# Sums of squares in a decoder layer: 128x128 blocks turned on TensorE and added on VectorE instead of float32 products with ones

## The chip, the cores and the metric

The kernel runs on one core of a Trainium2 chip. The metric is the device time of one execution in microseconds (us), and a version is judged by the median of its runs. The core has a matrix engine (TensorE, "PE" in the profile, with its weight loads shown apart as "PEld"), a vector engine (VectorE, "DVE"), a scalar engine (ScalarE, "ACT"), a general engine (GpSimd, "POOL") and a queue that mostly issues transfers (SyncE, "SP"). Each engine takes its instructions strictly in its own order, and they wait for one another by semaphores.

## What is computed

One layer of a decoder over 1024 tokens with 1024 features, all in float32:

```
x = x + 1/2 * SwiGLU_1(RMSNorm(x))
h = RMSNorm(x); z = h @ W_in      # [u | v | c_q | c_kv | k_rope | q_mem | gates]
merged = sum_i sigmoid(gate_i) * (y_i @ W_branch_i)     # gating, latent and memory attention
x = x + merged @ W_out
x = x + 1/2 * SwiGLU_2(RMSNorm(x))
```

What matters here are the root-mean-square norms, `x * rsqrt(mean(x*x) + EPS) * g`. Each needs, for every token, the sum of the squares over some features:

- over the 1024 features of `x`, in three places: before the first feed-forward block ("ffn1"), before the mixer's input projection ("mix") and before the second feed-forward block ("ffn2");
- over the 1024 features of the 256 memory tokens (`mem`);
- over the 128 features of each of four query heads of the memory attention (`q_mem`);
- over the 384 features of the low-rank query `c_q` (the kernel adds 256 of them at the place that is changed here, and the last 128 elsewhere).

## The kernel before

**Layout.** Activations lie feature by feature: a tile has 128 features on the partitions and tokens along the row, so the tokens are handled in two halves of 512. The sum over features runs across partitions. The squares are first added up, feature tile by feature tile, into one tile (128 features by tokens), and what remains is a sum over 128 partitions for each token.

**How that sum is made.** `token_sums` (line 391) does it on TensorE. For each block of 128 tokens it takes the 128x128 block of squares as the stationary operand and one column of ones (`self.ones`) as the moving one, in plain float32, and gets one column of 128 sums in a PSUM bank, one token on each partition. In the trace each such float32 product is recorded as two weight loads and two matmuls. `query_roots` (line 762) does the same with `self.pick`, a 128x2 matrix whose first column has ones in the upper 64 rows and whose second column has them in the lower 64, because its tile holds two heads of 64 summed features each. The sums go, straight from PSUM, into `rms` (line 206): nine small VectorE instructions (lines 192 and 169 to 185) that compute the reciprocal root.

**The way back.** Where the root has to multiply features-by-tokens tiles, `norm_scale` (line 405) spreads it with TensorE transposes (line 411): each takes a root column, broadcast to 128x128, as the stationary operand and the identity `self.ident` as the moving one. Transposes of this kind also occur in many other places (lines 436, 614, 818, 922, 1006, 1041).

**Main products.** All large products are split into three (`mm3`, lines 155 to 161): each float32 operand becomes a rounded high part and a rest, made by a ScalarE copy and a VectorE subtraction (lines 139 and 142; the profile also shows them as 146 and 147, and as 150 and 151 with a gain), and three matmuls of 512 columns (lines 158, 159, 160) are added in PSUM. A scheme with seven products in place of eight (class `Seven`) adds VectorE sums of weights (line 1411) and of results (line 1439).

**Order of the work.** Three kinds of stages matter:

- The ffn blocks' second half (`down`) and the first units after it run under an order written out by hand, for TensorE, VectorE and ScalarE, and in `down` for SyncE too.
- The input projection (`Gates.run`, line 1664) goes through fifteen units of seven products each. There only TensorE's order is written by hand; the other engines' order is made by a planner that simulates a timeline. After the first product of some units the table `sums` calls `mem_root` (unit 2), `query_roots` (units 7 and 10) and `latent_sums` (unit 12). The squares of these come from stored values that are read back, squared on ScalarE and added on GpSimd (`squares`, line 663), one unit or more earlier.
- The mixer and the output projection (`project`, line 1114) are planned throughout.

**PSUM.** There are eight banks of 512 columns: a ring of four called `bank` (line 135), which the sums use, and four more that `single` or `mm` use. Each unit of the projection takes one `bank` and two `single`.

**Who calls `token_sums`.** `OpNorm.tokens` (line 1288) for both halves of the three norms of `x` (with `late`, which puts the first matmul behind the latest main product in TensorE's order), `mem_root` with 2 blocks, `latent_sums` with 8. For the mix norm, `tokens(0)` and `root` stand ahead of step (5, 2) of `down`, and `turn`, which calls `norm_scale`, ahead of step (5, 3). For ffn2, `first` (line 1326) is called by `project` after the first output tile of the second half.

Of the kernel before, what the change touches and what calls it, by code (L numbers as in the profile page):

```python
# [8 lines left out]
F32 = mybir.dt.float32  # L9
# [4 lines left out]
ALU = mybir.AluOpType  # L14
AXX = mybir.AxisListType.X

P = 128
D = 1024
S = 1024
DT = D // P  # L20
NT = S // P
# [13 lines left out]
ML = 256  # L35
# [14 lines left out]
class Kernel:  # L50
# [193 lines left out]
    def late_constants(self):  # L244

        nc, a, const = self.nc, self.a, self.const

        def load(name, shape):
            t = const.tile(shape, F32, name="c_" + name)
            nc.sync.dma_start(t, a[name])  # L250
            return t

        self.b_gate = load("b_gate", [P, 3 * DT])
        self.g_mix, self.g_ffn2, self.g_mem = (load(n + "_norm", [P, DT]) for n in ("mix", "ffn2", "mem"))
        self.g_cq = load("mla_cq_norm", [P, QR // P])
        self.sg_b = load("sg_b", [P, SGG])
        self.mq_g = load("mem_q_norm", [P, 1])
        self.mk_g = load("mem_k_norm", [P, 1])
        self.gq_m = const.tile([P, 1], F32, name="gq_m")
        nc.gpsimd.tensor_scalar(self.gq_m, self.mq_g, -MD ** -0.5, None, op0=ALU.mult)  # L260
        self.pick = const.tile([P, 2], F32, name="pick")
        nc.gpsimd.memset(self.pick, 0.0)
        for o in range(2):
            nc.gpsimd.memset(self.pick[o * P // 2:(o + 1) * P // 2, o:o + 1], 1.0)
        self.g_ev = {}
        rope_g = {}
        for n in ("q", "k"):
            g = const.tile([QK, 1], F32, name=f"g_ev_{n}")
            nc.gpsimd.memset(g, 1.0)
            nc.sync.dma_start(g[:NOPE], a[f"mla_{n}_norm"][:NOPE].unsqueeze(1))  # L270
            self.g_ev[n] = g
            rope_g[n] = const.tile([P, ROPE], F32, name=f"rope_g_{n}")
            nc.sync.dma_start(rope_g[n], a[f"mla_{n}_norm"][NOPE:].partition_broadcast(P))
        pos = const.tile([P, NT], I32, name="pos_i")
        nc.sync.dma_start(pos, a["positions"])
        inv = const.tile([P, ROPE // 2], F32, name="inv")
        nc.sync.dma_start(inv, a["inv_freq"].partition_broadcast(P))
        yield
        yield from self.rope_tables(rope_g, pos, inv)
# [111 lines left out]
    def token_sums(self, acc, late=False, bank=None, more=()):  # L391


        n = acc.shape[-1] // P
        b = (bank or self.bank)()[:, :n]
        for t in range(n):
            for m, x in enumerate((acc, *more)):
                i = self.nc.tensor.matmul(
                    b[:, t:t + 1], x[:, t * P:(t + 1) * P], self.ones, start=m == 0, stop=m == len(more))
                if late and t == m == 0:  # L400
                    self.after(i, self.last)
        self.final = i
        return b

    def norm_scale(self, r, late=False, bank=None):


        n = r.shape[-1]
        b = (bank or self.bank)()
        for t in range(n):  # L410
            i = self.nc.tensor.transpose(
                b[:, t * P:(t + 1) * P], r[:, t:t + 1].to_broadcast([P, P]), self.ident)
            if late and t == 0:
                self.after(i, self.last)
        self.final = i
        return b[:, :n * P]
# [332 lines left out]
    def mem_root(self, t):  # L749

        v, row = self.nc.vector, self.row()
        v.tensor_tensor(row, t[:, :512], t[:, 512:], op=ALU.add)
        v.tensor_tensor(row[:, :ML], row[:, :ML], row[:, ML:], op=ALU.add)
        self.m_r = self.const.tile([P, ML // P], F32, name="m_r")
        v.tensor_copy(self.m_r, self.rms(self.token_sums(row[:, :ML]), ML // P, D))

    def query_squares(self, z, pair):

# [3 lines left out]
    def query_roots(self, pair, t):  # L762

        nc = self.nc
        b = self.bank()[:, :NT * 2]
        for n in range(NT):
            nc.tensor.matmul(b[:, 2 * n:2 * n + 2], t[:, n * P:(n + 1) * P], self.pick, start=True, stop=True)
        if pair == 0:
            self.mq_r, self.mq_nr = (
                self.const.tile([P, NT * MH], F32, name=n).rearrange("p (t h) -> p t h", h=MH) for n in ("mq_r", "mq_nr"))  # L770
        c = slice(2 * pair, 2 * pair + 2)
        nc.vector.tensor_copy(self.mq_r[:, :, c], self.rms(b, NT * 2, MD).rearrange("p (t h) -> p t h", h=2))
        nc.gpsimd.tensor_scalar(self.mq_nr[:, :, c], self.mq_r[:, :, c], -1.0, None, op0=ALU.mult)
# [5 lines left out]
    def latent_sums(self, t):  # L779

        self.cq_s = self.const.tile([P, NT], F32, name="cq_s")
        self.nc.vector.tensor_copy(self.cq_s, self.token_sums(t))

    def mem_rows(self):

# [466 lines left out]
class OpNorm:  # L1252
# [35 lines left out]
    def tokens(self, half):  # L1288
        k = self.k
        more, self.more = self.more, []  # L1290
        self.s[half] = k.token_sums(self.acc.pop(half), late=k.last is not None, more=more)

    def root(self, half):
        self.r[half] = self.k.rms(self.s[half], 4, D)
# [1005 lines left out]
```

## Time and profile before

| | |
|---|---|
| Median of 3 runs | 2167.88 us (2167.59 to 2170.26) |
| Profiled execution, first to last instruction | 2168.8 us (of this execution no other time is recorded) |
| Granted TensorE clock, mean | 0.999 |
| Busy TensorE / weight loads | 2159.0 us (100%) / 1804.2 us (83%) |
| Busy VectorE / ScalarE / GpSimd | 1567.5 us (72%) / 912.3 us (42%) / 256.9 us (12%) |
| DMA, mean share of 16 engines, on the hardware queue | 45.4% |

A row of the page or of a timeline gives the start, the duration, the engine, the line of the kernel, the operation, the output and inputs with their shapes, a count, and in brackets how long the engine stood idle before it and what released it. Matmuls overlap: the duration of one is longer than the distance from one start to the next, so what an insertion costs TensorE is read from the starts.

### The profile page before, as it was taken

The numbers are of one execution on the slowest core, as the hardware profiler recorded it, in microseconds if no ns is written. First come the engines' busy times: TensorE is split into PE (matmuls) and PEld (weight loads), VectorE is DVE, ScalarE is ACT, GpSimd is POOL, SyncE is SP. The second block draws the span as 40 slices with busy tenths as digits, with TensorE's granted clock in tenths as the row PEclk, the third lists the DMA queues.
The fourth block names the chain that finished last, engine by engine and source line by source line (L and its number), as shares of the span: only waits on it lengthen the run. The fifth ranks groups of instructions, "written<-read, shape, count | busy, mean of one in ns | idle before, by whom it ended". The sixth has DMA issues, their size and how long they took to land.

```text
span 2168.8 us, 27547 instructions
## 1 busy us (share of the span) xinstructions
PE 2159.0 (100%) x10170; PEld 1804.2 (83%) x10170; DVE 1567.5 (72%) x2362; ACT 912.3 (42%) x1492; POOL 256.9 (12%) x271
## 2 busy tenths in 40 slices
PE   9999999999999999999999999999999999999999
PEld 6888888888887888888888899988888888888887
DVE  7966666679889656655786679886886666657884
ACT  5433333333455434433555378833432232224332
POOL 0011111100000000000133321240011211110000
PEclk9999999999999999999999999999999999999999
DMA  4264555385332445641577821193033333338443
GB/s 147 92 219 160 187 180 175 123 319 189 123 116 100 145 164 174 223 148 61 209 279 260 312 101 60 51 354 110 34 132 102 103 99 99 108 138 289 169 130 104
DMA packets 129975, 340.98 MB, mean 157 GB/s; under 512 B 15280, under 2 KB 23600, under 8 KB 129840
## 3 DMA queue, kind: packets, MB, share of 16 engines
q1 hardware_dynamic: 129696, 339.21, 45.4%
q8 instruction: 80, 1.31, 0.2%
q14 instruction: 55, 0.45, 0.1%
q10 hardware_dynamic: 144, 0.00, 0.0%
HBM read 229.33 MB, written 109.84 MB: 156 GB/s over the span
## 4 chain that ended last, share of the span: by engine, by line
PE 93%; DVE 4%; ACT 1%; DMA 1%; issue 1%; SPq 0%; ACTq 0%; DVEq 0%
PE one L158 15%; PE one L159 15%; PE one L160 15%; PE bank L158 13%; PE bank L159 12%; PE bank L160 12%; PE mm L158 2%; PE mm L159 2%; PE mm L160 2%; PE bank L1006 1%; PE bank L1021 1%; PE bank L1022 1%; PE bank L436 1%; PE one L1935 1%; DVE w L147 1%; DVE wlo L147 1%
## 5 line engine op out<-in xcount | busy, mean ns | idle before, releaser
L146 ACT CAST whi<-x 128x1024 fp32r<-128x1024 f32 x202 | 192.2, 955 | 419.0 <-DVE x L1411 169.9
L147 DVE TENSOR_TENSOR wlo<-x,whi 128x1024 fp32r<-128x1024 f32 x202 | 241.1, 1195 | 58.8 <-ACT whi L146 21.0
L1439 DVE TENSOR_TENSOR t<-t,one 128x512 f32<-128x512 f32 x188 | 128.8, 685 | 195.2 <-PE one L160 195.1
L158 PE MATMUL bank<-h,whi 128*128 128x512 f32 x636 | 247.9, 390 | 0.0
L160 PE MATMUL bank<-h,wlo 128*128 128x512 f32 x636 | 247.6, 389 | 0.0
L159 PE MATMUL bank<-h,whi 128*128 128x512 f32 x636 | 247.6, 389 | 0.0
L158 PE MATMUL one<-h,whi 128*128 128x512 f32 x508 | 199.2, 392 | 0.0
L159 PE MATMUL one<-h,whi 128*128 128x512 f32 x508 | 198.2, 390 | 0.0
L160 PE MATMUL one<-h,wlo 128*128 128x512 f32 x508 | 198.2, 390 | 0.0
L158 PE MATMUL one<-w,whi 128*128 128x512 f32 x432 | 168.8, 391 | 0.1
L160 PE MATMUL one<-w,wlo 128*128 128x512 f32 x432 | 168.2, 389 | 0.0
L159 PE MATMUL one<-w,whi 128*128 128x512 f32 x432 | 168.1, 389 | 0.0
L142 DVE TENSOR_TENSOR wlo<-w,whi 128x1024 fp32r<-128x1024 f32 (+2 forms) x112 | 114.4, 1037 | 67.1 <-ACT whi L139 66.9
L139 ACT CAST whi<-w 128x1024 fp32r<-128x1024 f32 (+2 forms) x112 | 98.8, 902 | 149.8 <-PE one L159 63.9
L2035 POOL TENSOR_TENSOR raw<-raw 128x512 f32<-128x512 f32 x38 | 56.9, 1498 | 794.1 <-DVE raw L1876 684.1
L160 PEld LDWEIGHTS bank<-h,wlo 128*128 128x128 f32 x636 | 119.4, 188 | 24.9
L158 PEld LDWEIGHTS bank<-h,whi 128*128 128x128 f32 x636 | 119.4, 188 | 24.6
L159 PEld LDWEIGHTS bank<-h,whi 128*128 128x128 f32 x636 | 119.4, 188 | 24.4
L160 PE MATMUL bank<-whi,wlo 128*128 128x512 f32 x352 | 137.0, 389 | 0.0
L158 PE MATMUL bank<-whi 128*128 128x512 f32 x352 | 137.0, 389 | 0.0
L159 PE MATMUL bank<-wlo,whi 128*128 128x512 f32 x352 | 137.0, 389 | 0.0
L158 PEld LDWEIGHTS one<-h,whi 128*128 128x128 f32 x508 | 95.8, 189 | 20.0 <-issue 0.2
(406 smaller groups left out, 4904.7 us busy)
## 6 DMA issues: line engine op xcount, KB each, us to landing
x<-in_ffn_w_gu_dram SPq DMA_DIRECT2D x78, 512.0 KB, 5.1
w<-tdt SPq DMA_DIRECT2D x40, 512.0 KB, 4.5
gate<-raw SPq DMA_DIRECT2D x33, 512.0 KB, 2.9
tdb<-raw SPq DMA_DIRECT2D x64, 256.0 KB, 2.3
h<-in_ffn_w_down_dram SPq DMA_DIRECT2D x64, 256.0 KB, 6.2
w<-tdb SPq DMA_DIRECT2D x30, 512.0 KB, 4.6
tdt<-w SPq DMA_DIRECT2D x48, 256.0 KB, 2.3
x<-in_w_gate_dram SPq DMA_DIRECT2D x22, 512.0 KB, 7.0
```

Source lines behind the costliest of these rows:

```text
L139: i = self.nc.scalar.copy(hi, src)
L142: return (eng or self.nc.vector).tensor_tensor(lo, src, hi.bitcast(F32), op=ALU.subtract)
L146: self.nc.scalar.copy(hi, src)
L147: return lambda: self.nc.vector.tensor_tensor(lo, src, hi.bitcast(F32), op=ALU.subtract)
L158: i = mmul(out, s[0], m[0], start=first, stop=False, **kw)
L159: mmul(out, s[0], m[1], start=False, stop=False, **kw)
L160: self.last = mmul(out, s[1], m[0], start=False, stop=last, **kw)
L436: nc.tensor.transpose(b[:m, k * P:(k + 1) * P], s, self.ident)
L1006: nc.tensor.transpose(b[:, at:at + P], prs[t][:, kk * P:(kk + 1) * P], self.ident)
L1021: nc.tensor.matmul(o, w, pt[0], start=n == 0, stop=False)
L1439: return self.nc.vector.tensor_tensor(out, x, y, op=ALU.add)
L2035: sub = lambda d, x, y: (eng or nc.gpsimd).tensor_tensor(d, x, y, op=ALU.subtract)
```

## The change

A new helper, `turned_sums`, takes the place of the float32 products in five calls: `mem_root` (2 blocks), the two calls of `query_roots` (8 blocks each), `latent_sums` (8 blocks), and `tokens(0)` of the mix norm and of the ffn2 norm (4 blocks each). Each 128x128 block of squares is transposed on TensorE into a PSUM bank, four blocks to a bank, and one VectorE reduction for each bank adds along the row: over 128 features, or over twice 64 for the query heads (`parts=2`). The sums now lie in an SBUF tile ("ts"). Eight blocks take two banks where they took one. The ffn1 norm, whose object is made with `scaled=True`, and `tokens(1)` of the other two keep `token_sums`. `self.pick` and its three GpSimd memsets go.

```diff
-        self.pick = const.tile([P, 2], F32, name="pick")
-        nc.gpsimd.memset(self.pick, 0.0)
-        for o in range(2):
-            nc.gpsimd.memset(self.pick[o * P // 2:(o + 1) * P // 2, o:o + 1], 1.0)
...
+    def turned_sums(self, acc, parts=1, late=False):
+        nc, n = self.nc, acc.shape[-1] // P
+        out = self.stat("ts", NT * 2)[:, :n * parts]
+        for t0 in range(0, n, 4):
+            m = min(4, n - t0)
+            b = self.bank()
+            for t in range(m):
+                i = nc.tensor.transpose(b[:, t * P:(t + 1) * P], acc[:, (t0 + t) * P:(t0 + t + 1) * P], self.ident)
+                if late and t0 == t == 0:
+                    self.after(i, self.last)
+            nc.vector.tensor_reduce(
+                out[:, t0 * parts:(t0 + m) * parts],
+                b[:, :m * P].rearrange("p (x d) -> p x d", d=P // parts), axis=AXX, op=ALU.add)
+        self.final = i
+        return out
...
-        v.tensor_copy(self.m_r, self.rms(self.token_sums(row[:, :ML]), ML // P, D))
+        v.tensor_copy(self.m_r, self.rms(self.turned_sums(row[:, :ML]), ML // P, D))
...
-        b = self.bank()[:, :NT * 2]
-        for n in range(NT):
-            nc.tensor.matmul(b[:, 2 * n:2 * n + 2], t[:, n * P:(n + 1) * P], self.pick, start=True, stop=True)
+        b = self.turned_sums(t, 2)
...
-        self.nc.vector.tensor_copy(self.cq_s, self.token_sums(t))
+        self.nc.vector.tensor_copy(self.cq_s, self.turned_sums(t))
...
-        self.s[half] = k.token_sums(self.acc.pop(half), late=k.last is not None, more=more)
+        if half == 0 and not self.scaled:
+            self.s[half] = k.turned_sums(self.acc.pop(half), late=True)
+        else:
+            self.s[half] = k.token_sums(self.acc.pop(half), late=k.last is not None, more=more)
```

## The prediction

> **What bounds the kernel now.** I read the page's sums first, then the chain of work that ended last, then what TensorE waits for.
>
> ```profile
> span 2168.8 us, 27547 instructions
> PE 2159.0 (100%) x10170; PEld 1804.2 (83%) x10170; DVE 1567.5 (72%) x2362; ACT 912.3 (42%) x1492; POOL 256.9 (12%) x271
> ...
> PE 93%; DVE 4%; ACT 1%; DMA 1%; issue 1%; SPq 0%; ACTq 0%; DVEq 0%
> ```
>
> ```profile
> PE bank L231 <- POOL pick L264: 1.5, 1, 1.5
> PE bank L1935 <- DVE x L1911: 1.2, 2, 0.7
> ...
> PE bank L411 <- DVE rs_y L185: 0.7, 1, 0.7
> ```
>
> TensorE is busy for all but 9.8 us of the span, and 93% of the chain runs through it. The first wait is the start of the program; the one at line 411 is at a half norm that the change leaves alone. So what shortens TensorE's own list of instructions shortens the time, as long as no other engine becomes late. By stage (columns: stretch, length, busy time and count of PE, PEld, DVE, ACT and POOL, clock, DMA share, GB/s), the input projection and, for later use, the two parts of the mixer:
>
> ```profile
> 700.00:960.00 260.00, 259.91 (x1175) 215.64 (x1174) 162.40 (x229) 106.83 (x132) 10.96 (x6) 1.00 0.51 173
> ...
> 1060.00:1240.00 180.00, 179.43 (x991) 158.05 (x990) 137.13 (x285) 92.82 (x228) 55.55 (x62) 1.00 0.77 277
> 1240.00:1420.00 180.00, 179.24 (x1216) 162.98 (x1215) 151.42 (x317) 137.48 (x304) 42.36 (x96) 1.00 0.28 102
> ```
>
> In the projection, where 26 of the 34 replaced blocks are, TensorE has 0.1 us of idle time in 260, and VectorE has 98 us to spare.
>
> **What is removed.** 34 blocks: 2 (memory), 8 and 8 (queries), 8 (latent), 4 (mix norm), 4 (ffn2 norm). Of each, two recorded matmuls go. The query sums (line 767) and the latent sums (the whi form of line 398):
>
> ```profile
> L767 PE MATMUL bank<-pick,whi x32: 165/251/252, 850.3 to 911.1; 128*128 128x2 f32 x32
> ...
> L398 PE MATMUL bank<-ones,whi x16: 164/250/251, 949.4 to 951.0; 128*128 128x1 f32 x16
> ```
>
> The durations overlap, so I go by the starts of TensorE's main matmuls around a place. The first query sum:
>
> ```profile
> 848.05 0.39 PE L160 MATMUL bank<-h,wlo 128*128 128x512 f32 x1
> ...
> 850.09 0.39 PE L160 MATMUL bank<-h,wlo 128*128 128x512 f32 x1
> ...
> 850.32 1.84 PE L767 MATMUL bank<-pick,whi 128*128 128x2 f32 x16
> ...
> 852.58 0.40 PE L160 MATMUL one<-w,wlo 128*128 128x512 f32 x1
> ```
>
> From 848.05 to 850.09 lie nine ordinary steps, 0.227 us each. From 850.09 to 852.58, 2.49 us, lie three, so the eight blocks cost 2.49 - 0.68 = 1.81 us, 0.226 a block. I take the third main matmul behind the insertion because the first two come late by some 0.1 us. The mix norm has four blocks, and soon after it four transposes:
>
> ```profile
> 602.03 0.39 PE L160 MATMUL one<-whi,wlo 128*128 128x512 f32 x1
> 602.26 0.95 PE L398 MATMUL bank<-ones,t 128*128 128x1 f32 x8
> ...
> 603.62 0.40 PE L160 MATMUL one<-whi,wlo 128*128 128x512 f32 x1
> ...
> 608.42 0.39 PE L160 MATMUL one<-whi,wlo 128*128 128x512 f32 x1
> 608.65 0.60 PE L411 MATMUL bank<-ident,rs_y 128*128 128x128 f32 x4
> ...
> 609.56 0.40 PE L160 MATMUL one<-whi,wlo 128*128 128x512 f32 x1
> ```
>
> In the same way, four products with ones cost 1.59 - 0.68 = 0.91 us (0.228 a block). Removed in all: 2 x 0.227 + 3 x 1.81 + 2 x 0.91 = **7.70 us**.
>
> **What TensorE gets instead.** Four transposes cost 1.14 - 0.68 = 0.46 us in the rows above, 0.115 a block. A longer row of them, with data as the stationary operand as here, is at line 614:
>
> ```profile
> 1130.33 0.40 PE L159 MATMUL mm<-wlo,h 128*128 128x512 f32 x1
> 1130.57 1.91 PE L614 MATMUL bank<-ident,h 128*128 128x128 f32 x16
> ...
> 1132.79 0.40 PE L159 MATMUL mm<-wlo,h 128*128 128x512 f32 x1
> ```
>
> Sixteen cost 2.46 - 0.68 = 1.78 us, 0.111 a block. Eight lie between, 0.89 to 0.92; I take 0.90. Added in all: 2 x 0.115 + 3 x 0.90 + 2 x 0.46 = **3.85 us**. TensorE's list gets shorter by 7.70 - 3.85 = 3.85 us; with 0.111 or 0.115 for every block it would be 3.9 or 3.8.
>
> [...] In the attention, full of transposes, the row by stage shows a granted clock of 1.00.
>
> **What VectorE gets.** Nine reductions out of PSUM: two each for the three sums of eight blocks, one each for the norms, one of half the size. Reductions of the trace, the first out of SBUF, the second out of PSUM:
>
> ```profile
> L481 DVE TENSOR_REDUCE qk_ss<-raw x8: 670/677/685, 1071.1 to 1110.1; 128x8 f32<-128x512 f32 x8
> ...
> L862 DVE TENSOR_REDUCE m_mx<-mm x8: 1214/1218/1226, 1151.9 to 1191.9; 128x4 f32<-128x1024 f32 x8
> ```
>
> 512 columns take 0.68 us by the first and half of 1.22 by the second, 0.61; I take 0.68, so 8 x 0.68 + 0.34 = 5.8 us in all. I cost this at nothing; the cover is this. At the query sums VectorE stands in front of the first root instruction and waits for TensorE:
>
> ```profile
> 852.20 0.17 DVE L192 TENSOR_SCALAR rms_v<-bank 128x16 f32<-128x16 f32 x1 [2.09 <-PE bank L767]
> ...
> 855.15 0.69 DVE L1439 TENSOR_TENSOR t<-t,one 128x512 f32<-128x512 f32 x1 [0.90 <-PE one L160]
> ...
> 857.60 0.39 PE L158 MATMUL one<-w,whi 128*128 128x512 f32 x1
> ```
>
> The 2.09 us of waiting become two reductions. The first four transposes end some 0.5 us after 850.3, the reductions then run to about 852.1, and the root starts where it started. Behind it the queue holds the sum at line 1439, and TensorE waits for that: its next product adds onto the same `single` bank. That sum ends at 855.84 and the product starts at 857.60, a cover of 1.76 us. TensorE arrives 0.9 us sooner after the change; the sum, which waits 0.90 us for TensorE now, can come as much sooner, so the cover stays. If the reductions took 1.8 us each instead of 0.68, some 2.2 us more in all, it would be gone, and each place would cost the excess. The latent place is the same with less behind it.
>
> At the mix norm, VectorE's order is by hand:
>
> ```profile
> 603.24 0.16 DVE L192 TENSOR_SCALAR rms_v<-bank 128x4 f32<-128x4 f32 x1 [2.10 <-PE bank L398]
> ...
> 604.83 0.16 DVE L185 SCALAR_TENSOR_TENSOR rs_y<-rs_w,rs_y 128x4 f32<-128x4 f32 x1
> 604.91 2.42 DVE L142 TENSOR_TENSOR wlo<-w,whi 128x512 fp32r<-128x512 f32 x3
> ```
>
> The reduction starts 0.45 us before 603.24 and takes 0.68, so the root and the three splits behind it end 0.2 us later: at 605.2 and 607.5. TensorE wants the root for the transposes at 608.43 and the splits at about 609.2, both 0.45 sooner, so 2.8 and 1.2 us remain. At ffn2:
>
> ```profile
> 1494.69 0.94 PE L398 MATMUL bank<-ones,t 128*128 128x1 f32 x8
> ...
> 1498.15 0.16 DVE L185 SCALAR_TENSOR_TENSOR rs_y<-rs_w,rs_y 128x4 f32<-128x4 f32 x1
> ...
> 1501.08 0.60 PE L411 MATMUL bank<-ident,rs_y 128*128 128x128 f32 x4
> ```
>
> The root ends at 1498.31, 0.68 later if the reduction lies in front of it, against 1500.6: still 1.6 us.
>
> **The rest.** The second bank of an eight-block sum comes from a ring of four whose earlier owners were read a unit ago; if it brings one more wait event on TensorE's queue, that is 51 ns by the events at the query sums, three times, 0.15 us at most:
>
> ```profile
> L767 PEldq EVENT_SEMAPHORE  x3: 51/51/51, 846.3 to 905.6; - x3
> ```
>
> The three memsets of `pick` go from GpSimd's first two microseconds; TensorE's warm-up, released there, is followed by a wait for the first data, so they are worth nothing. No transfer is issued, moved or dropped. For all of this I take 0, between a loss of 0.15 us and a gain of 0.1.
>
> **Sum.** 2168.8 - 3.85 = 2164.95 us for a profiled execution. The median of the runs is 0.9 us below the profiled span, so 2167.88 - 3.85 = **2164.0 us**. A difference below 0.2% (4.3 us) cannot be told from none in this kernel, and 3.85 is 0.18%: the forecast itself sits at that edge.
>
> **Rivals.** (a) *The planner's other order helps.* In projection, mixer and output projection the order on VectorE, ScalarE, GpSimd and SyncE is planned from simulated times, which the change alters. The most that a lucky order can give is TensorE's idle time there, by the rows by stage 0.1 + 0.6 + 0.8 = 1.5 us, so 2162.5. For it: the stages from 700 to 1500 us are nearly all in the planner's hands. Against it: it would have to find nearly all of that.
>
> (b) *The sums come late.* VectorE is held longer than I think at the three eight-block places, because it cannot start on the first bank before both are filled or the planner puts the reductions behind other work, and TensorE waits about 1.2 us at each: 3.6 of 3.85 us are given back, 2167.6. Against it: the 1.76 us of cover.
>
> (c) *Slower: the planned order in the attention gets worse.* There VectorE is busy for 151 and ScalarE for 137 of 180 us, while TensorE has 0.8 us idle over 32 steps of scores, turning and values. One vector operation put ahead of a split that TensorE needs next costs what that operation takes:
>
> ```profile
> L142 DVE TENSOR_TENSOR wlo<-bank,whi 128x512 fp32r<-128x512 f32 x64 | 42.2, 679 | 5.6 <-ACT whi L139 2.6 <-POOL wlo L1011 2.1 <-issue 0.7
> ```
>
> At 0.68 us in every second step it is 10.9 us: 2164.0 + 10.9 = 2174.9. It takes the gain away from the sixth such step on, and shows as slower from the twelfth. Against it: nothing in that stage is edited.
>
> (d) *The transposes run as plain float32 products with the identity*, so the change does not do what it says. The warm-up's products of that kind are recorded twice each and take 3.6 us for nine, 0.40 each; 34 would cost 13.6 in place of 3.85, so 2173.8. Against it: the transposes at line 818 are recorded once each:
>
> ```profile
> L231 PE MATMUL bank<-ident x18: 275/421/582, 1.5 to 5.0; 128*128 128x128 f32 x18
> ...
> L818 PE MATMUL mm<-ident,h x8: 271/272/273, 1136.8 to 1137.6; 128*128 128x128 f32 x8
> ```
>
> (e) *A transpose costs TensorE its whole recorded duration*, 0.272 us by the row above: 34 x 0.272 = 9.25, a loss of 1.55 us, 2169.4. Against it: the sixteen at line 614. [...]
>
> **How the numbers follow.** Forecast 0.70, (a) 0.12, (b) 0.08, (c) 0.07, (d) 0.01, (e) 0.02. The forecast's own range is 2163.0 to 2165.0: 0.15 for the bank waits, and the rest for how well two medians of such runs agree. The range that holds 8 in 10 reaches towards (a) and (b), 2161.3 to 2168.0. Faster by over 0.2% means below 2163.5: a third of the forecast (0.23) and (a), 0.35. Slower by over 0.2%: (c) and (d), 0.08. The rest, 0.57, is no difference that can be told.
>
> **What would show it.** Right: 34 transposes in 26 + 8 blocks, recorded once each; from the last main matmul before to the third after the eight of a query sum 1.58 us instead of 2.49; reductions of 0.6 to 0.7 us directly behind the transposes; TensorE's idle time as before; every later stage earlier by the sum up to there, 0.45 us from 610 on, 3.4 us from 960, 3.85 at the end. Wrong: a new wait of TensorE for lines 142, 147, 1439 or 185; a drift that begins in a stage without an edit; a clock below 1.00 around the transposes.

## The result, and the profile after

The changed kernel takes 2164.41 us (median of 16 runs, 2163.42 to 2165.85). The kernel before, run beside it, takes 2169.55 us (median of 16, 2167.59 to 2170.26). The ratio is 0.9978 with a 95% interval of 0.9972 to 0.9985, so 4.8 us less, and between 3.3 and 6.1 us (the two medians alone differ by 5.1). The forecast was 2164.0 us and 3.85 us less. It named a difference below 4.3 us as one that cannot be told from none, and put most of its chance there; the result lies just beyond that mark, and its interval reaches below it.

The changed kernel's 16 runs fall into two groups some 1.3 us apart, 11 with a mean granted clock of 1.000 (mean 2164.08 us) and 5 with 0.999 (2165.31), and those of the kernel before split alike in the later batches (the lower and the upper group, below).

The profiled execution of the changed kernel went from 2168.8 to 2161.7 us of span, 7.1 us. On the page of the kernel after, the span, the busy TensorE and the chain of work that ended last:

```profile
span 2161.7 us, 27485 instructions
PE 2152.9 (100%) x10136; PEld 1798.9 (83%) x10136; DVE 1571.5 (73%) x2371; ACT 911.7 (42%) x1492; POOL 259.1 (12%) x268
...
PE 94%; DVE 4%; ACT 1%; issue 1%; DMA 0%; POOL 0%; ACTq 0%; POOLq 0%; DVEq 0%
```

TensorE is idle for 8.8 us in place of 9.8, VectorE has nine instructions and 4 us more, and the chain still runs through TensorE. The three longest waits of TensorE (what waited, for what; total us, times, longest) and the row of the projection in the view by stage:

```profile
PE bank L231 <- POOL ident masks.py:199: 1.5, 1, 1.5
PE one L158 <- DVE raw L1454: 0.9, 2, 0.7
PE bank L425 <- DVE rs_y L185: 0.7, 1, 0.7
```

```profile
700.00:960.00 260.00, 260.00 (x1162) 215.13 (x1161) 166.83 (x236) 107.71 (x132) 12.44 (x6) 1.00 0.51 175
```

No new wait of over 0.2 us has come, the projection has no idle TensorE, and its clock is 1.00. The new instructions, grouped (duration min/median/max in ns, first and last start):

```profile
L410 PE MATMUL bank<-ident,whi x24: 270/272/273, 847.4 to 945.4; 128*128 128x128 f32 x24
L410 PE MATMUL bank<-ident,t x10: 271/272/273, 600.2 to 1488.5; 128*128 128x128 f32 x10
L413 DVE TENSOR_REDUCE ts<-bank x9: 425/683/692, 600.8 to 1488.9; 128x4 f32<-128x512 f32 x4, 128x8 f32<-128x512 f32 x4, 128x2 f32<-128x256 f32 x1
```

34 transposes, each recorded once, and nine reductions of 0.68 us (0.43 for the half-size one). The timeline at the first query sum, TensorE:

```profile
847.15 0.40 PE L160 MATMUL bank<-h,wlo 128*128 128x512 f32 x1
847.39 1.03 PE L410 MATMUL bank<-ident,whi 128*128 128x128 f32 x8
...
848.73 0.39 PE L160 MATMUL one<-w,wlo 128*128 128x512 f32 x1
```

and VectorE:

```profile
848.02 1.29 DVE L413 TENSOR_REDUCE ts<-bank 128x8 f32<-128x512 f32 x2 [0.86 <-PE bank L410]
...
851.27 0.69 DVE L1454 TENSOR_TENSOR t<-t,one 128x512 f32<-128x512 f32 x1 [0.49 <-PE one L160]
```

From 847.15 to 848.73 are 1.58 us where 2.49 were. VectorE's wait of 2.09 us is now one of 0.86 us and two reductions, and the sum at line 1454 (line 1439 before) still waits for TensorE, not TensorE for it.

**Where the 7.1 us lie.** I matched the matmuls of two traces in their order and read how far the starts had moved at each place. Against the first profile of before, the edited places do not account for 7.1 us. The largest other shift is in the first feed-forward block, behind its half norm of 24 recorded products with ones. The view by stage (columns as in the prediction; the clock is third from the end) and then TensorE's timeline there, kernel before:

```profile
36.00:46.00 10.00, 10.00 (x53) 8.56 (x52) 7.78 (x16) 2.71 (x4) 0.00 (x0) 0.83 0.00 0
```

```profile
36.34 2.85 PE L398 MATMUL bank<-ones,t 128*128 128x1 f32 x24
39.62 0.63 PE L159 MATMUL one<-h,whi 128*128 128x512 f32 x1
40.05 0.63 PE L160 MATMUL one<-h,wlo 128*128 128x512 f32 x1
```

and the same two views of the kernel after:

```profile
36.00:46.00 10.00, 10.00 (x59) 8.69 (x58) 9.21 (x18) 4.22 (x5) 0.00 (x0) 1.00 0.00 0
```

```profile
35.80 2.73 PE L394 MATMUL bank<-ones,t 128*128 128x1 f32 x24
38.72 0.39 PE L159 MATMUL one<-h,whi 128*128 128x512 f32 x1
38.94 0.39 PE L160 MATMUL one<-h,wlo 128*128 128x512 f32 x1
```

In the first the matmuls start 0.43 us apart and last 0.63 us, for some 3 us; the granted clock in that window is 0.83. In the second they start 0.23 us apart at a clock of 1.00. Line 398 is the old `token_sums`, which the change leaves in place here. The change therefore could not be credited with this, unless it had moved something that far ahead; the experiments decide that.

### The profile page after: what moved, and what is told of

The parts are those of the page before. It is cut to its first block, busy times and chain, and to the rows that moved or that the text cites. A ratio compares the mean times of both kernels' runs of the same rounds, so it can differ in the third digit from the quotient of the medians.

```text
span 2161.7 us, 27485 instructions
## 1 busy us (share of the span) xinstructions
PE 2152.9 (100%) x10136; PEld 1798.9 (83%) x10136; DVE 1571.5 (73%) x2371; ACT 911.7 (42%) x1492; POOL 259.1 (12%) x268
## 4 chain that ended last, share of the span: by engine, by line
PE 94%; DVE 4%; ACT 1%; issue 1%; DMA 0%; POOL 0%; ACTq 0%; POOLq 0%; DVEq 0%
PE one L158 15%; PE one L159 15%; PE one L160 15%; PE bank L158 13%; PE bank L159 13%; PE bank L160 13%; PE mm L158 2%; PE mm L159 2%; PE mm L160 2%; PE bank L1018 1%; PE bank L1033 1%; PE bank L1034 1%; PE bank L450 1%; DVE wlo L147 1%; PE bank L1950 1%; PE one L1950 1%
## 5 line engine op out<-in xcount | busy, mean ns | idle before, releaser
L160 PEld LDWEIGHTS one<-h,wlo 128*128 128x128 f32 x508 | 95.3, 188 | 19.9
```

The costliest lines, as they stand in the source:

```text
L160: self.last = mmul(out, s[1], m[0], start=False, stop=last, **kw)
```

## The experiments

### The kernel before, profiled again

No edit.

> The kernel before, profiled once more. Theory (the first profile's 7.1 us of difference are 3.85 us of the edit, 1.5 us of a half-clock stretch behind the 24 products with ones at 36 to 39 us that only a part of the runs of either kernel has, and a few tenths of transfers that land earlier or later): a span between 2166 and 2169 us; where its granted clock is 1.000 the products at 39 to 42 us start 0.227 us apart and the span is some 1.5 us shorter than 2168.8; where it is 0.999 they start 0.43 us apart. The first product's start (9.6 us) and the wait for the transfer whi<-wks at 1068 us (0.4 us) may come out otherwise by some tenths. Rival (the stretch belongs to the kernel before as such, and the edit takes it away): a clock of 0.999 and the same stretch, in this profile and in every other of this kernel.

Measured: 2168.02 us, span 2166.3, granted clock 1.000. The same two views:

```profile
36.00:46.00 10.00, 10.00 (x60) 8.69 (x59) 9.22 (x18) 4.22 (x6) 0.00 (x0) 1.00 0.00 0
```

```profile
35.98 2.73 PE L398 MATMUL bank<-ones,t 128*128 128x1 f32 x24
38.88 0.39 PE L159 MATMUL one<-h,whi 128*128 128x512 f32 x1
39.11 0.40 PE L160 MATMUL one<-h,wlo 128*128 128x512 f32 x1
```

So the kernel before also runs without the half-clock stretch, and the rival falls. This second profile is the one to compare with the profile after. The table gives, for each profile, by how much the starts of TensorE's matmuls move against it within a stretch of time (us; stretches that are left out add at most 0.03). It is worked out from the starts in the traces, each mark by the median of seven neighbouring matmuls, and not a view of the profile.

```
stretch (us, before)       before   after   again   twice reduce4  halves rounded roundall
start to 32                  0.37   -0.18   -0.18   -0.07    0.16   -0.07   -0.07   -0.66
32 to 46, ffn1 half norm     1.59   -0.04    1.56   -0.05    0.00    0.01    1.57   -1.35
46 to 590                   -0.17   -0.10   -0.36    0.02   -0.05   -0.03   -0.10    0.27
590 to 612, mix norm         0.00   -0.50   -0.50   -0.07   -0.50   -0.47   -0.47   -0.47
612 to 748                   0.08   -0.06    0.24   -0.10    0.08    2.86    0.07    0.02
748 to 765, memory          -0.04   -0.24   -0.23   -0.02   -0.24   -0.23   -0.23   -0.24
846 to 857, query 1          0.00   -0.95   -0.92   -0.05   -0.95   -0.93   -0.89   -0.89
905 to 916, query 2          0.00   -0.95   -0.96   -0.08   -0.96   -0.95   -0.90   -0.89
916 to 945                   0.00    0.00    0.00    0.00    1.04    0.00    0.00    0.00
945 to 957, latent           0.00   -0.96   -0.95   -0.08   -0.95   -0.95   -0.89   -0.90
957 to 1480                  0.56   -0.21   -0.17    1.75   -0.06   -0.16    0.01   -0.02
1480 to 1500, ffn2 norm      0.00   -0.49   -0.50   -0.07   -0.47   -0.49   -0.45   -0.46
1500 to 2160                 0.05    0.06    0.03    0.02    0.04    1.24    0.04   -0.43
whole                        2.44   -4.62   -2.94    1.20   -2.83   -0.16   -2.31   -6.03
```

("before" is the first profile, "again" the second of the changed kernel.) The change takes hold at six places, one for each of its calls (the count of five calls given above is one short). In the column of the kernel after, they sum to 0.50 + 0.24 + 0.95 + 0.95 + 0.96 + 0.49 = 4.09 us out of 4.62. The remaining 0.53 us are scattered, none over 0.21.

### The changed kernel, once more

No edit. It ran on one chip with three of the runs below: each transpose twice, all blocks by float32r products, and part of the long row moved forward. The other four below ran on a second chip, beside more runs of the kernel before.

> The changed kernel, as the measure for the other runs on the same chip. By TensorE's list: 3.85 to 4 us below the kernel before (ratio 0.9982), whatever the group of runs. The runs of both kernels fall in two groups about 1.5 us apart; theory of the clock: the upper group has a stretch of some 3 us at half clock behind the twelve products with ones of the ffn1 norm (which the change leaves alone), as the profile before shows at 39 to 42 us; a profile of the lower group has none.

Measured: 2163.99 us (11 runs, 2163.57 to 2165.40), ratio 0.9977 [0.9968, 0.9985]. Six runs lie between 2163.57 and 2163.99 us at a clock of 1.000, five between 2164.83 and 2165.40 at 0.999. The profile was one of the five, and its window from 36 to 46 us has a clock of 0.83:

```profile
36.00:46.00 10.00, 10.00 (x51) 8.50 (x51) 7.82 (x17) 2.75 (x4) 0.00 (x0) 0.83 0.00 0
```

The half-clock stretch is thus in the changed kernel too, in a part of its runs, and costs 1.6 us of its profile (column "again"). The runs beside it of the kernel before split 14 to 14 by the same clocks, with means of 2168.64 and 2169.97 us. Group by group the change is worth 4.89 us (2163.75 against 2168.64) and 4.84 (2165.13 against 2169.97).

### Each transpose twice

```diff
-                i = nc.tensor.transpose(b[:, t * P:(t + 1) * P], acc[:, (t0 + t) * P:(t0 + t + 1) * P], self.ident)
+                for _ in range(2):
+                    i = nc.tensor.transpose(b[:, t * P:(t + 1) * P], acc[:, (t0 + t) * P:(t0 + t + 1) * P], self.ident)
...
```

> Each of the 34 transposes is issued twice, into the same place; nothing else changes. Theory (the gain is the difference in TensorE's list, 0.114 us a block): 34 x 0.111 = 3.8 us above the changed kernel, so within 0.3 us of the kernel before (ratio to it 0.9999), and 0.89 us more between the main matmuls around a sum of eight blocks. Rival (the gain came from another order of the planned stages or from a freer VectorE): within 1 us of the changed kernel, ratio to before 0.998.

Measured: 2168.95 us (11 runs), ratio 0.9998 [0.9989, 1.0007]: the gain is gone. At the first query sum:

```profile
847.97 0.40 PE L160 MATMUL bank<-h,wlo 128*128 128x512 f32 x1
848.21 1.91 PE L411 MATMUL bank<-ident,whi 128*128 128x128 f32 x16
...
850.42 0.40 PE L160 MATMUL one<-w,wlo 128*128 128x512 f32 x1
```

Sixteen transposes take 2.45 us from main matmul to main matmul, less 0.68 for three steps 1.77, as the sixteen at line 614 did. In the table the six places sum to -0.37 us, so the 34 extra transposes cost 4.09 - 0.37 = 3.72 us, **0.109 each**, and a block by products with ones 0.109 + 4.09/34 = 0.229 us. That is the price of the trade, measured by doubling it. The column's other shift, 1.75 us between 957 and 1480, is not at an edited place. Some 0.5 us of it come at 1430 us; 1.3 us come at 1067 us, where TensorE waited for the read-back of weights from memory:

```profile
PE mm L158 <- DMA whi<-wks: 1.2, 1, 1.2
```

That transfer lands within tenths of when TensorE wants it. In the first profile of before TensorE's weight load waited 0.4 us for it, in the one of after not at all. Group by group the run lies 4.8 and 4.0 us above the changed kernel (2168.58 and 2169.17 us), more than the theory's 3.8; the excess is of the size of that shift, so that the time equals the kernel before's is in part chance, and the price rests on the six places.

### Four reductions for one

```diff
-            nc.vector.tensor_reduce(
+            for _ in range(4 if n == 8 else 1):
+                nc.vector.tensor_reduce(
```

> The changed kernel with each reduction of the eight-block sums (two query places, one latent place: six instructions) made four times, so that VectorE has 6 x 0.68 = 4.1 us more at each of the three places and TensorE's list is the changed kernel's. Theory (the reductions are free because they lie under cover): the forecast put the cover left at a query place at some 2.2 us, so of 4.1 us about 1.9 us come out at each of the two query places, and nothing or up to 1.9 us at the latent place, whose sum is not needed at once: 3.8 to 5.7 us over the changed kernel, some 2168 to 2170 us beside its 2164.0, with a new wait of TensorE for a tile of VectorE after each query sum. Rival (VectorE's list is slack here however long it is): within 0.5 us of the changed kernel. Second rival (the reductions were never under cover): 12 us over it, all of the added work.

Measured: 2166.66 us (11 runs), ratio 0.9987 [0.9978, 0.9995]. Against the changed kernel's groups the runs are 1.7 us longer in the lower (2165.42) and 1.8 in the upper (2166.93); measured from the kernel before on each of the two chips (here 2168.81 and 2170.26) it is 1.5 in both. So of 12.3 us of extra VectorE work (18 x 0.68) 1.5 to 1.8 us come out; the theory had said 3.8 to 5.7, the rivals 0.5 and 12. All three are off, and the theory's mechanism is half right. VectorE and TensorE behind the second query sum:

```profile
906.86 3.68 DVE L414 TENSOR_REDUCE ts<-bank 128x8 f32<-128x512 f32 x6 [0.85 <-PE bank L410]
910.45 0.68 DVE L1455 TENSOR_TENSOR t<-t,one 128x512 f32<-128x512 f32 x1
...
911.65 1.28 DVE L414 TENSOR_REDUCE ts<-bank 128x8 f32<-128x512 f32 x2
...
914.05 0.17 DVE L192 TENSOR_SCALAR rms_v<-ts 128x16 f32<-128x16 f32 x1
...
918.16 0.68 DVE L1455 TENSOR_TENSOR t<-t,one 128x512 f32<-128x512 f32 x1
...
918.89 0.50 PE L158 MATMUL one<-h,whi 128*128 128x512 f32 x1 [0.74 <-DVE t L1455]
```

The planner does not hold the queue in the order that I took as fixed: it sets the sum of line 1455 ahead of the last two reductions and the whole root behind it. The first sum after the place is in time; TensorE is caught one unit later, by 0.74 us of waiting and 1.04 us of shift, at the second place only. Some 0.4 us more lie outside the span, in each of its runs (2165.62 us for a span of 2163.5, where the other runs have 1.7 us more than their span); why is open. At the first query place and at the latent place nothing came out. The cover exists, it is finite, and here it was much larger than the 1.76 us that I read off one interval.

### The other two half norms turned as well

```diff
-        if half == 0 and not self.scaled:
+        if not self.scaled:
             self.s[half] = k.turned_sums(self.acc.pop(half), late=True)
```

> The changed kernel with the other two half norms (second halves of the mix norm and of the second feed-forward layer's norm) turned too: eight blocks more by transposes in place of products with ones, two reductions more of 0.68 us. Theory of covers: TensorE's list is shorter by 2 x 0.46 = 0.9 us, but both sums stand in front of a root that TensorE already waits for, so VectorE's chain is longer by 0.68 us at each and the wait takes the 0.46 us back: about 0.2 us a place longer, 2164.0 + 0.4 = 2164.4 us, with TensorE's wait for rs_y longer by some 0.7 us. Rival (TensorE's list alone sets the time): 0.9 us less, 2163.1 us.

Measured: 2169.27 us (11 runs), ratio 0.9998 [0.9989, 1.0007]; five runs between 2167.23 and 2167.93 at a clock of 0.999, six between 2169.27 and 2169.86 at 0.998, none at 1.000. Both theories were far too low. The timeline of VectorE and TensorE at the mix norm's second half:

```profile
654.17 0.69 DVE L413 TENSOR_REDUCE ts<-bank 128x4 f32<-128x512 f32 x1 [0.53 <-PE bank L410]
654.77 1.22 DVE L147 TENSOR_TENSOR wlo<-x,whi 128x1024 fp32r<-128x1024 f32 x1
655.91 0.17 DVE L192 TENSOR_SCALAR rms_v<-ts 128x4 f32<-128x4 f32 x1
...
657.71 0.65 PE L425 MATMUL bank<-ident,rs_y 128*128 128x128 f32 x4 [2.19 <-DVE rs_y L185]
...
659.48 0.63 PE L159 MATMUL one<-h,h 128*128 128x512 f32 x1
659.91 0.63 PE L160 MATMUL one<-h,h 128*128 128x512 f32 x1
```

The stage in the kernel after, and in this one:

```profile
640.00:670.00 30.00, 29.19 (x135) 23.72 (x134) 28.82 (x48) 13.16 (x18) 0.00 (x0) 1.00 0.24 88
```

```profile
640.00:670.00 30.00, 27.65 (x118) 22.05 (x117) 28.30 (x48) 11.27 (x15) 0.00 (x0) 0.94 0.24 88
```

Two things were missing from the theory. The split of 1.22 us stands between the reduction and the root, so the root begins 1.05 us after the reduction ends; in the kernel after the same split ran from 653.36 to 654.59 us, mostly while TensorE was still at the products with ones (653.08 to 654.13). And TensorE, which waited 2.19 us, came back to half clock: from 659 us the matmuls start 0.43 us apart, for 3.4 us. In the table this place costs 2.86 us in all, and at the ffn2 norm, where the wait is 1.52 us and the clock stays at 1.00, the loss is 1.24. The six runs at 0.998 would fit a second half-clock stretch, at the ffn1 norm; none of them was profiled. This is the converse of the forecast's step on cover: the same exchange loses where TensorE takes up the root as soon as it is there.

### A longer row of products with ones

```diff
-                i = self.nc.tensor.matmul(
-                    b[:, t:t + 1], x[:, t * P:(t + 1) * P], self.ones, start=m == 0, stop=m == len(more))
+                for z in range(3 if more and m == 0 else 1):
+                    i = self.nc.tensor.matmul(
+                        b[:, t:t + 1], x[:, t * P:(t + 1) * P], self.ones, start=m == 0, stop=m == len(more),
+                        skip_group_check=True)
...
```

> The changed kernel with the products of acc with ones in the second half of the first feed-forward layer's norm made three times: eight products more, 8 x 0.226 = 1.8 us. Theory of the clock (the row of products with ones there lets TensorE's clock fall to half for some 3 us afterwards, in a part of the runs only, which splits them in two groups about 1.3 us apart): with a longer row the fall comes in every run; none is left in the lower group, the median is 2164.0 + 1.8 + 1.3 = 2167.1 us, and the products behind the row start 0.43 us apart in the profile. Rival (the two groups come from elsewhere): 2164.0 + 1.8 = 2165.8 us with both groups as before.

Measured: 2168.14 us (11 runs, 2167.31 to 2169.58), ratio 0.9996 [0.9987, 1.0005]. Every run has a clock of 0.999 or 0.998. TensorE's timeline behind the row, and the view by stage:

```profile
36.33 4.52 PE L395 MATMUL bank<-ones,t 128*128 128x1 f32 x40
...
42.24 0.63 PE L160 MATMUL one<-h,wlo 128*128 128x512 f32 x1
42.66 0.63 PE L158 MATMUL one<-h,whi 128*128 128x512 f32 x1
```

```profile
36.00:46.00 10.00, 10.00 (x61) 8.85 (x60) 6.05 (x15) 1.98 (x3) 0.00 (x0) 0.83 0.00 0
```

With 4.5 us of ones no run of 11 is left at a clock of 1.000, and the profiled one has the stretch; with 2.7 us the upper group of the changed kernel has 5 of 16 and 5 of 11 runs, that of the kernel before 14 of 28. The theory's 2167.1 us was 1.0 short of the median, and the rival's 2165.8 and its two groups fall. Why four runs went to 0.998 is open.

### All 58 blocks by float32r products with two columns

These are the 34 and 24 more: 4 and 12 at the two half norms of ffn1, and 4 at each of the other two (the expectation counts 20 in place of 24, and 54 in all). The squares are stored rounded to float32r, so each sum is one of rounded squares. That is a change in what is added, not only in how.

```diff
+        self.pair = {n: const.tile([P, 2], F32R, name=f"pair{n}") for n in (1, 2)}
...
-                    b[:, t:t + 1], x[:, t * P:(t + 1) * P], self.ones, start=m == 0, stop=m == len(more))
+                    b[:, 2 * t:2 * t + 2], x[:, t * P:(t + 1) * P].bitcast(F32R), self.pair[1],
+                    start=m == 0, stop=m == len(more))
...
-            k.nc.scalar.activation(sq[:, n], x[:, n], ACT.Square)
+            k.nc.scalar.activation(sq[:, n].bitcast(F32R), x[:, n], ACT.Square)
```

> All sums of squares, the ffn1 norm and the second halves too, as products with ones in the rounded float32 form of the main products (float32r) in place of float32 products or transposes; two columns of ones, no reduction on VectorE. The squares are rounded to that form as they are written, which makes the sums less exact. Theory (what costs is the number of weight loads of a block, two in float32, one in float32r or for a transpose): the 34 blocks cost as much as the transposes; 20 further blocks save 0.113 each, 2.3 us; the ffn1 sums take 1.4 us instead of 2.7, so that the half clock goes too. 2.3 to 3.2 us below the changed kernel, about 2161.5. Rival (float32r with a moving operand of two columns is slow, or its weight load costs two): no better than the kernel before.

Measured: 2162.36 us (6 runs, 2162.02 to 2162.91), ratio 0.9969 [0.9957, 0.9981], every run at a clock of 1.000. It is the fastest version here, 1.6 us below the changed kernel's median on that chip and 1.3 below its lower group, short of the theory's 2.3 to 3.2. TensorE's timeline at a sum of eight blocks:

```profile
845.84 0.39 PE L160 MATMUL bank<-h,wlo 128*128 128x512 f32 x1
846.06 0.95 PE L415 MATMUL bank<-pair,whi 128*128 128x2 f32 x8
...
847.43 0.40 PE L160 MATMUL one<-w,wlo 128*128 128x512 f32 x1
```

Eight blocks cost 1.59 - 0.68 = 0.91 us, as by transposes, and need no reduction. The table shows 0.66 us saved up to the first half norm of ffn1 (against 0.18 in the kernel after), 1.35 at its second and 0.43 at that of ffn2, nothing at that of the mix norm, and 0.27 us given back between 46 and 590. There TensorE, which is now earlier, waits at 70 us for a sum of VectorE, by its waits:

```profile
PE one L158 <- DVE raw L1457: 1.4, 2, 1.3
```

With half the products in the row, the clock is 1.000 in each of the six runs, which agrees with the run with the longer row.

### The same 34 blocks by float32r products

As above, for the 34 turned blocks alone; the other 24 keep the float32 products with ones. Here too the squares are rounded.

> The changed kernel with its 34 turned blocks summed in another way: the squares are stored rounded (float32r), and a block's sum is one product with two columns of ones, with no reduction on VectorE. Theory (what counts at a block is the 128x128 weights, loaded once by a transpose and by a float32r product, twice by a float32 product; and the reductions are covered): the same as the changed kernel within 0.5 us, 2164.0 us. Rival (the reductions cost time): less by up to 9 x 0.68 = 6.1 us; already the run with all 54 blocks of this kind, at 2162.4 us, speaks against most of that. Rival (the transposes cost less than such a product): up to 3.9 us more, 2167.9 us, the price of the products taken out.

Measured: 2165.25 us (11 runs, 2164.30 to 2165.84), ratio 0.9980 [0.9972, 0.9989]. Five runs at 1.000 have a mean of 2164.46, six at 0.999 one of 2165.60, that is 0.7 and 0.5 us over the changed kernel's on the other chip, and 0.5 and 0.2 when each is measured from the kernel before on its own chip. In the table the six places sum to 3.83 us against 4.09. So a block costs (4.09 - 3.83) / 34 = 0.008 us more this way than by a transpose, and taking 5.8 us of reductions off VectorE gains nothing. Both rivals fall, and the theory's 0.5 us about holds.

### Part of the long row moved forward

Of the 24 recorded products with ones in the ffn1 half norm, sixteen were moved between the first products, to shorten the row.

```diff
-            rows(1, range(DT))
+            rows(1, (0, 1, 2))
+            norm.early(0)
+            rows(1, (3, 4, 5))
+            norm.early(1)
+            rows(1, (6, 7))
...
```

> The changed kernel, in which eight of the twelve products with ones of the ffn1 norm's second half stand earlier, four behind the third and four behind the sixth feature tile of the first products, into columns of their own; VectorE adds the three columns of each token with one small reduction. Same work on TensorE. Theory (a run of 2.7 us of products with ones lets the clock fall to half for some 3 us in a part of the runs): no run has the stretch at half clock, the runs no longer split, the upper group vanishes; and the root starts some 0.6 us sooner, of which 0.4 arrive behind VectorE. 0.4 us below the lower group of the changed kernel, 0.8 to 1.2 below its median. Rival (the half clock comes at a chance moment of the start, whatever runs there): the runs split as before.

Measured: 2171.56 us (11 runs), ratio 1.0012 [1.0004, 1.0021]: not faster, for a reason of its own. TensorE's timeline, and the view by stage:

```profile
31.14 1.47 PE L1316 MATMUL bank<-ones,t 128*128 128x1 f32 x8 [3.89 <-ACT t L1285]
32.47 8.35 PE L1975 MATMUL one<-x,w 128*128 128x512 f32 x12
```

```profile
32.00:42.00 10.00, 10.00 (x25) 5.02 (x26) 6.55 (x8) 3.54 (x5) 0.00 (x0) 0.68 0.01 2
```

The first group waited 3.89 us for a square of ScalarE, and behind the wait the clock in the window is 0.68: it is at half from 31.60 to 38.42 us. The run says nothing on a shorter row, since it put a wait in its place. Here the wait cost more than its length: behind 3.89 us of it came 6.82 us at half clock.

## Why the prediction was right

**What bounds the kernel.** Right. TensorE's list sets the time: 34 transposes more took 3.72 us at the same places, and most of the extra VectorE work did not show.

**What is removed, what TensorE gets.** The two terms were 7.70 and 3.85 us; by the doubled transposes they are 34 x 0.229 = 7.8 and 3.7. The difference, 3.85 in the forecast, is 4.09 us at the six places. A query sum came out at 1.58 us, as forecast, and the whole shift behind it is 0.95 and not 0.91: the third main matmul behind a row has not quite settled, and later ones move 0.04 us more. Rivals (d) and (e) are excluded: each transpose is recorded once, and the duration of 0.272 us costs 0.109 on TensorE's list.

**What VectorE gets.** The reductions took 0.68 us and cost nothing, as forecast. The size of the cover was wrong. The step "if the reductions took some 2.2 us more in all it would be gone, and each place would cost the excess" counted the root as fixed ahead of line 1439's sum. With 4.1 us more the planner put root steps behind that sum, and the loss was 1.04 us at one place of three. At the mix norm the root ended at 603.26 us, 3.06 us after the row of transposes began, where it was 2.73 us after the row of products; no wait for it appeared:

```profile
603.10 0.16 DVE L185 SCALAR_TENSOR_TENSOR rs_y<-rs_w,rs_y 128x4 f32<-128x4 f32 x1
```

**The rest and the rivals.** No wait on a bank appeared. Rival (a) has some support: between 957 and 1480 us the profiles of after are earlier by 0.21 and 0.17 us without an edit, two tenths out of its 1.5. The forecast named such a drift as a sign of being wrong; it is there, but small. That the planner's order is the cause is argued, not shown. Rivals (b) and (c) did not occur.

**The sum.** The step that was mis-sized is the time from which it starts. "The median of the runs is 0.9 us below the profiled span" set a median of three runs against one profile with the half-clock stretch in it. Each profiled execution of the later runs, other than the one with more reductions, took 1.7 to 1.8 us more than its own span. By that the first profile's execution took about 2168.8 + 1.7 = 2170.5 us, and the median of the kernel before over 16 runs is 2169.55, not 2167.88. From 2169.55 the forecast's 3.85 us lead to 2165.7, 1.3 us above what was measured. So 2164.0 came so close by luck: a start that was 1.7 us too low and a gain that was too small offset each other. Of what the gain lacked, 0.24 us are at the edited places and 0.5 us in small shifts elsewhere. The rest is how many runs of each kernel fell in the upper group: with five of 16 after, and about half of the kernel before's in the later batches, (0.5 - 0.3) x 1.3 = 0.3 us. Group by group the change is worth 4.8 to 4.9 us in the runs and 4.62 in the profiles without the stretch; what makes up the last 0.2 us is not settled.

## What to carry to other kernels

Where float32 sums over partitions stood on TensorE's path, turning the blocks and adding on another engine halved their price here, from 0.229 to 0.109 us a block, as long as nobody waited for the sum; where TensorE took the result up at once, the same edit lost, 2.86 and 1.24 us at the two places, by the reduction, by what stood behind it in the queue, and at the first by the clock after the wait. A product in float32r with two columns had nearly the transposes' price, 0.008 us a block more, without the reductions, if rounded squares will do. Before a profile's span is set beside a median, look for stretches with a lower granted clock in the rows by stage: one of 3.4 us moved the profile here by 1.59 us, a third of the change's 4.62.

## What the runs showed of the hardware

**Behind a row of one-column float32 products TensorE went to half clock although it was never idle** (in the first profile of before it was busy for 10.00 us of the 10 from 36 to 46, at a clock of 0.83). Behind 2.7 us of such products the matmuls started 0.43 us apart for about 3 us in some profiles (before, after_again) and 0.23 us apart in others (after, before_again). Behind 4.5 us they started 0.43 us apart in the one profile, and no run of 11 had a clock of 1.000; behind a row of half as many products, in float32r, all six runs had a clock of 1.000. The same came behind a wait of 2.19 us, for 3.4 us, and not behind one of 1.52 us. The loss is some 1.3 us in the runs (1.23 and 1.38 between the two groups of the changed kernel) and 1.6 in the profiles (1.56 to 1.59).

**Why only in some runs: the falls lay on steps of 3.413 us.** The clock records in the traces date the stretch. In the first profile of before the clock rose to full 4.69 us after the first instruction, fell to half at 38.82 and rose again at 42.24 us. In all four profiles that have the stretch behind the row (before, after_again, rounded, long) it lasts 3.413 us and begins 34.133 us, ten times that, after the clock first rose to full, which happened between 4.6 and 7.5 us after the first instruction. Counted in such steps, the last step ahead of the fall held 2.48 to 2.73 us of the row (2.48 in the first profile of before). In the profiles without a fall at the row, no step held more than 1.96 us of it (1.96 in the one of after, 1.40 with float32r). The falls behind the waits of the runs with turned half norms and with the row moved forward come on such steps too, the 191st and the 7th, and so do the falls at the end of the program, the 634th in the first profile of before (at 2168.74 us) and the 632nd in the one of after (at 2163.08). So where the row lies between two steps, which differs from run to run, fits as what decides; no run moved the row by itself to test it.

**Whether transposes do this is open.** Sixteen in a row, 1.77 us, left the clock at 1.00 (845 to 857 us, each transpose twice); but so did the rows of products with ones at the query sums, 1.84 us (700 to 960 us, kernel before), and longer rows of transposes were not tried.
